# Batch norm with ReLU on one core: two stores of the first tile cut at row 6 instead of row 8

## The chip, the core and the metric

The kernel runs on one core of a Trainium2 chip. The metric is the device time of one execution in microseconds (us); the median of several executions is given with its extremes. All executions quoted here are in the fast state. A ratio is the mean time of one kernel's fast runs over the mean time of the other's fast runs in the same rounds on the same chip, so it is not quite the ratio of the medians quoted beside it.

## The reference

```python
# x: 32 x 128 x 32 x 32, float32; the other inputs: 128 numbers each
normalized = (x - running_mean[None, :, None, None]) / np.sqrt(running_var[None, :, None, None] + eps)
scaled = normalized * gamma[None, :, None, None] + beta[None, :, None, None]
return np.maximum(scaled, 0).astype(np.float32)
```

x has 16.78 MB, and so has the result. Each element is read once and written once.

## The kernel before

Batch and channel are laid out together as 4,096 images of 1,024 numbers (HW in the code). Two tiles (t = 0 and 1) hold 128 partitions x 16 rows; a row is one image, 4 KB in a partition. A channel's scale and bias are worked out once, and one ScalarE activation per row applies them with the ReLU, in place. SyncE, written SP, issues all loads in the first 8.5 us (queue q1). ScalarE issues the stores between its activations (queue q10).

```python
# (t, first row, row after the last): one SBUF tile and one load each, unless LOAD_CUTS cuts the load
TILES = ((0, 0, 2), (0, 2, 4), (0, 4, 8), (0, 8, 16), (1, 0, 16))
LOAD_CUTS = {(1, 8)}
STORE_CUTS = {(0, 1)}
HALVES = {(1, 0), (1, 1)}          # rows whose activation is done in two halves
# ...
with tc.manual_schedule(engines={mybir.EngineType.Activation}):
    for t, a, b, xt in tiles:
        first = a
        for j in range(a, b):
            step = HW // 2 if (t, j) in HALVES else HW
            for w in range(0, HW, step):
                nc.scalar.activation(
                    out=xt[:, j - a, w : w + step], in_=xt[:, j - a, w : w + step], func=ACTF.Relu,
                    bias=bias_t[:, j : j + 1], scale=scale_t[:, j : j + 1],
                )
            if j + 1 == b or (t, j + 1) in STORE_CUTS:
                nc.scalar.dma_start(
                    out=outr[t, :, first : j + 1, :], in_=xt[:, first - a : j + 1 - a, :]
                )
                first = j + 1
```

The rows of one store lie side by side in a partition and in memory, so a store of n rows moves one packet of n x 4 KB per partition. There are 128 packets per store, 8 for each of the 16 DMA engines.

## Time and profile before

| | before |
|---|---|
| time, median of 3 runs | 83.47 us (83.46 to 83.57) |
| span of the instructions in the profile | 81.7 us |
| ScalarE busy | 48% |
| load queue + store queue, share of 16 engines | 48.6% + 47.8% |
| first load packet starts / last store packet ends (packet records) | 1.82 / 80.56 us |

The 16 DMA engines together are called the pipe here. A pipe that carries packets from 1.8 us to 80.6 us and is busy for 96.4% of the span has no idle time in between. Where a text here says "packet records", it means the start, duration and size of each single DMA packet in the trace.

### The profile page before, as it was taken

The numbers are of one execution on the slowest core, as the hardware profiler recorded it, in microseconds if no ns is written. First come the engines' busy times: TensorE is split into PE (matmuls) and PEld (weight loads), VectorE is DVE, ScalarE is ACT, GpSimd is POOL, SyncE is SP. The second block draws the span as 40 slices with busy tenths as digits, with TensorE's granted clock in tenths as the row PEclk, the third lists the DMA queues.
The fourth block names the chain that finished last, engine by engine and source line by source line (L and its number), as shares of the span: only waits on it lengthen the run. The fifth ranks groups of instructions, "written<-read, shape, count | busy, mean of one in ns | idle before, by whom it ended". The sixth has DMA issues, their size and how long they took to land.

```text
span 81.7 us, 128 instructions
## 1 busy us (share of the span) xinstructions
PE 1.7 (2%) x6; PEld 1.5 (2%) x6; DVE 0.8 (1%) x5; ACT 39.1 (48%) x36; POOL 0.8 (1%) x6
## 2 busy tenths in 40 slices
PE   0008000000000000000000000000000000000000
PEld 0007000000000000000000000000000000000000
DVE  0000300000000000000000000000000000000000
ACT  0600477799039999199997199993000000000000
POOL 3000000000000000000000000000000000000000
DMA  2899999989899898969789699996991999998290
GB/s 44 313 422 481 409 481 417 497 369 497 369 385 481 375 491 357 541 293 605 321 373 589 273 489 393 513 497 273 513 770 64 449 513 513 513 513 385 128 513 0
DMA packets 1793, 33.56 MB, mean 411 GB/s; under 512 B 257, under 2 KB 257, under 8 KB 513
## 3 DMA queue, kind: packets, MB, share of 16 engines
q1 hardware_dynamic: 864, 16.78, 48.6%
q10 hardware_dynamic: 928, 16.78, 47.8%
q14 instruction: 1, 0.00, 0.0%
HBM read 16.78 MB, written 16.78 MB: 411 GB/s over the span
## 4 chain that ended last, share of the span: by engine, by line
DMA 56%; ACT 10%; issue 2%; SPq 0%
DMA x<-in_x_dram 56%; ACT x L105 10%; SPq L56 0%
## 5 line engine op out<-in xcount | busy, mean ns | idle before, releaser
L105 ACT ACTIVATE x<-x,bias_t,scale_t 128x1024 f32<-128x1024 f32 (+1 forms) x34 | 37.5, 1178 | 10.0 <-DMA x<-in_x_dram 7.7
L89 ACT ACT_TABLE_LOAD x1 | 1.3, 1283 | 2.7 <-issue 2.7
L89 ACT ACTIVATE std_t<-cols,eps_t 128x16 f32<-128x16 f32 x1 | 0.3, 276 | 4.2 <-PE cols L81 4.2
L81 PE MATMUL cols<-raw,rep 8*128 8x16 f32 (+1 forms) x6 | 1.7, 384 | 6.4 <-DMA raw<-in_gamma_dram 6.3
L81 PEld LDWEIGHTS cols<-raw,rep 8*128 8x128 f32 x6 | 1.5, 307 | 6.5 <-issue 6.3
L68 POOL TENSOR_SCALAR_AFFINE_SELECT rep<-rep 8x128 f32<-8x128 f32 x1 | 0.4, 394 | 0.1
L91 DVE RECIPROCAL rstd_t<-std_t 128x16 f32<-128x16 f32 x1 | 0.3, 253 | 7.5 <-ACT std_t L89 7.5
L67 POOL MEMSET rep<- 8x128 f32 x1 | 0.2, 195 | 0.3 <-POOLq L133 0.3
L93 DVE TENSOR_TENSOR scale_t<-cols,rstd_t 128x16 f32<-128x16 f32 x1 | 0.2, 174 | 0.1
L95 DVE TENSOR_TENSOR ms_t<-cols,scale_t 128x16 f32<-128x16 f32 x1 | 0.2, 174 | 0.0
L97 DVE TENSOR_TENSOR bias_t<-cols,ms_t 128x16 f32<-128x16 f32 x1 | 0.2, 174 | 0.0
L133 POOL MEMSET const-bfloat16-1.0<- 128x1 bf16 x1 | 0.1, 108 | 0.0
L133 POOL MEMSET const-float32-0.0<- 128x1 f32 x1 | 0.1, 105 | 0.3 <-issue 0.3
L133 POOL MEMSET const-uint8-127<- 128x1 uint8 x1 | 0.1, 107 | 0.0
L133 POOL MEMSET const-float32-1.0<- 128x1 f32 x1 | 0.1, 105 | 0.0
L65 DVE MEMSET eps_t<- 128x1 f32 x1 | 0.1, 59 | 0.9 <-PEq L133 0.9
## 6 DMA issues: line engine op xcount, KB each, us to landing
x<-in_x_dram SPq DMA_DIRECT2D x3, 4096.0 KB, 38.6
out_dram<-x ACTq DMA_DIRECT2D x1, 4096.0 KB, 28.6
x<-in_x_dram SPq DMA_DIRECT2D x2, 1024.0 KB, 5.8
x<-in_x_dram SPq DMA_DIRECT2D x1, 2048.0 KB, 11.3
out_dram<-x ACTq DMA_DIRECT2D x1, 2048.0 KB
out_dram<-x ACTq DMA_DIRECT2D x2, 512.0 KB, 19.1
out_dram<-x ACTq DMA_DIRECT2D x1, 1024.0 KB
raw<-in_running_var_dram ACTq DMA_DIRECT2D x1, 0.5 KB
```

What stands on the lines that cost most here:

```text
L65: nc.vector.memset(eps_t, float(eps))
L67: nc.gpsimd.memset(rep, 1.0)
L68: nc.gpsimd.affine_select(out=rep, in_=rep, compare_op=mybir.AluOpType.is_equal, fill=0.0, base=0, pattern=[[0, P // Q], [-1, Q]], channel ...
L81: nc.tensor.matmul(cols[:, a:b, :].rearrange("p k j -> p (k j)"), rep.rearrange("q r s -> q (r s)"), raw[:, a:b, :].rearrange("q k j -> q ...
L89: nc.scalar.activation(out=std_t, in_=cols[:, 0, :], func=ACTF.Sqrt, bias=eps_t[:, 0:1], scale=1.0)
L91: nc.vector.reciprocal(out=rstd_t, in_=std_t)
L93: nc.vector.tensor_mul(out=scale_t, in0=cols[:, 1, :], in1=rstd_t)
L95: nc.vector.tensor_mul(out=ms_t, in0=cols[:, 2, :], in1=scale_t)
L97: nc.vector.tensor_sub(out=bias_t, in0=cols[:, 3, :], in1=ms_t)
L105: nc.scalar.activation(out=xt[:, j - a, w : w + step], in_=xt[:, j - a, w : w + step], func=ACTF.Relu, bias=bias_t[:, j : j + 1], scale=sc ...
L133: nc = _bacc.Bacc("TRN2", target_bir_lowering=False, num_devices=1)
```

## The change

Its intent can be read from the sizes: smaller packets for the store that may meet the last loads, and larger ones for the store that follows. Rows 4 to 15 become one tile, still loaded in two transfers, and its stores are cut after row 5.

```diff
-TILES = ((0, 0, 2), (0, 2, 4), (0, 4, 8), (0, 8, 16), (1, 0, 16))
+TILES = ((0, 0, 2), (0, 2, 4), (0, 4, 16), (1, 0, 16))

-LOAD_CUTS = {(1, 8)}
-STORE_CUTS = {(0, 1)}
+LOAD_CUTS = {(0, 8), (1, 8)}
+STORE_CUTS = {(0, 1), (0, 6)}
```

## The prediction

> **What bounds the kernel now.** I read the page first, then the DMA queues stretch by stretch, then the instructions of ScalarE in order of time.
>
> The page's first two parts, with the queues and the chain:
>
> ```profile
> span 81.7 us, 128 instructions
> ...
> PE 1.7 (2%) x6; PEld 1.5 (2%) x6; DVE 0.8 (1%) x5; ACT 39.1 (48%) x36; POOL 0.8 (1%) x6
> ...
> q1 hardware_dynamic: 864, 16.78, 48.6%
> q10 hardware_dynamic: 928, 16.78, 47.8%
> ...
> DMA 56%; ACT 10%; issue 2%; SPq 0%
> ```
>
> ScalarE, the busiest engine, works 48% of the span. The two DMA queues (q1 loads, issued by SP; q10 stores, issued by ScalarE) keep the 16 DMA engines busy for 48.6 + 47.8 = 96.4% of 81.7 us, which is 78.8 us. The chain gives DMA only 56% because it follows the last instruction of an engine (it ends at 55.9 us with ScalarE), not the store that lands afterwards. So I ask where the other 2.9 us are. The busy time of each stretch, with the DMA share as the last column but one:
>
> ```profile
> core 0: us, PE busy (x) PEld busy (x) DVE busy (x) ACT busy (x) POOL busy (x), PEclk, DMA share, GB/s
> 0.00:1.80 1.80, 0.00 (x0) 0.00 (x0) 0.06 (x1) 0.00 (x0) 0.80 (x6) 1.00 0.00 0
> 1.80:12.10 10.30, 1.75 (x6) 1.49 (x6) 0.78 (x4) 3.76 (x4) 0.00 (x0) 1.00 1.01 407
> ...
> 14.50:46.80 32.30, 0.00 (x0) 0.00 (x0) 0.00 (x0) 24.23 (x24) 0.00 (x0) 1.00 1.01 430
> 46.80:56.00 9.20, 0.00 (x0) 0.00 (x0) 0.00 (x0) 9.12 (x8) 0.00 (x0) 1.00 0.99 427
> 56.00:80.50 24.50, 0.00 (x0) 0.00 (x0) 0.00 (x0) 0.00 (x0) 0.00 (x0) 1.00 0.99 428
> 80.50:81.70 1.20, 0.00 (x0) 0.00 (x0) 0.00 (x0) 0.00 (x0) 0.00 (x0) 1.00 0.00 0
> ```
>
> The share is 0.99 to 1.01 from 1.8 us to 80.5 us; all that is idle is 1.8 us before the first load packet and 1.2 us after the last store packet. (A packet is booked where it starts, hence values a little over 1.) The kernel is a full DMA pipe from one end to the other. A change of store cuts pays only by fewer bytes, fewer or cheaper packets, or by closing a hole, and there is no hole.
>
> Next the packet price. The page counts 1,793 packets, one per partition and row range plus small ones. With stores alone in the pipe, the queue lines of two windows, 46.8 to 51 us (rows 4 to 7, 16 KB each) and 62 to 80 us (the last store, 64 KB each):
>
> ```profile
> DMA packets 112, 1.84 MB, mean 437 GB/s; under 512 B 0, under 2 KB 0, under 8 KB 0
> q10 hardware_dynamic: 112, 1.84, 101.8%
> ...
> DMA packets 112, 7.34 MB, mean 408 GB/s; under 512 B 0, under 2 KB 0, under 8 KB 0
> q10 hardware_dynamic: 112, 7.34, 94.0%
> ```
>
> 1.018 x 4.2 us x 16 / 112 = 0.611 us for a 16 KB packet, and 0.940 x 18 us x 16 / 112 = 2.417 us for one of 64 KB. The trace's single packet records agree and give all sizes of the store queue: 4 KB 0.159, 8 KB 0.309, 16 KB 0.611, 32 KB 1.213, 64 KB 2.418 us. The line from 32 to 64 KB has a slope of 1.205 us per 32,768 bytes (27.2 GB/s an engine, 435 GB/s for 16), and leaves about 0.008 us per packet whatever its size.
>
> **What the Trainium skill says.** "DMA: Bandwidth & Descriptors", section "Where 436 GB/s comes from", puts the ceiling of 16 engines at 435.2 GB/s; the slope above is that figure, so the bytes already flow at the ceiling. The same page, section "Queues, rings and completion order", says that each engine round-robins between its queue rows one packet at a time. The trace agrees: while loads of 32 KB and stores of 4 KB share the pipe (26 to 34 us), q1 has 88 packets at 82.8% and q10 has 89 at 11.1%: one for one by number, so a store's share grows with its packet. This is the one mechanism by which other cuts could move the loads. Section "Why small descriptors are slow (HBM only)" gives a fixed cost per packet; here it is the 0.008 us above, negligible from 4 KB up.
>
> **The change part by part.** The instruction streams of the two programs compare so: ScalarE keeps 34 activations and 6 stores, SP its 6 loads with the same sizes (2 x 8, 16, 3 x 32 KB a partition). Rows 4 to 15 become one tile loaded by two transfers; the activation of row 8 alone waits for the second, so the first four rows do not wait longer. Two things move: the store of 16 KB packets, issued after row 7, becomes one of 8 KB packets issued after row 5; that of 32 KB becomes 40 KB, issued after row 15 as before. One SP wait changes: the load of tile 1's first half waits for the beta load instead of the mean load before it is issued.
>
> *Bytes and packets.* Each engine sends 8 packets per store. Before: 8 x (0.611 + 1.213) = 14.59 us. After: 8 x 0.309 = 2.47 us for rows 4 and 5, and 8 x (40,960 bytes / 27.2 GB/s + 0.008) = 8 x 1.514 = 12.11 us, together 14.58 us. Difference: 0.01 us, nothing. The packets number 128 x 2 in both.
>
> *Order in the pipe.* The instructions of ScalarE in order of time:
>
> ```profile
> 15.61 4.63 ACT L105 ACTIVATE x<-x,bias_t,scale_t 128x1024 f32<-128x1024 f32 x4 [0.42 <-ACT x L105]
> 20.27 0.34 ACTq L113 DMA_DIRECT2D out_dram<-x  x1
> 23.84 9.16 ACT L105 ACTIVATE x<-x,bias_t,scale_t 128x1024 f32<-128x1024 f32 x8 [3.59 <-DMA x<-in_x_dram]
> 33.02 0.34 ACTq L113 DMA_DIRECT2D out_dram<-x  x1
> ...
> 46.77 9.16 ACT L105 ACTIVATE x<-x,bias_t,scale_t 128x1024 f32<-128x1024 f32 x8 [2.27 <-DMA x<-in_x_dram]
> 55.95 0.34 ACTq L113 DMA_DIRECT2D out_dram<-x  x1
> ```
>
> The store of rows 4 to 7 is issued at 20.27 us, but in the packet records its first packet starts at 46.35 us, 26 us later. Until then the store queue works through row 0 (from 14.56 us), row 1 (to 34.56 us) and rows 2 and 3 (36.56 to 46.69 us), one packet of theirs for each 32 KB load packet. The last load packets end at 46.07 us. So the two re-cut stores start where the loads end. Issuing rows 4 and 5 at about 18 us instead of 20.27 gains nothing, because they stand behind rows 0 to 3 either way; and their packets meet no load packet that they could push aside. Everything up to 46.4 us should stay, including the landing at 46.77 us that releases the last eight activations.
>
> *ScalarE.* One store issue moves from after row 7 to after row 5: about 0.4 us earlier in the list (0.34 us for the issue and the gap round it). Rows 6 and 7 end 0.4 us later, near 20.6 us; the next load lands at 23.8 us, so the 3.59 us of idle time absorb it. The issue at 33.02 us stays.
>
> *After the loads.* Before, from 46.69 us: 14.59 us of stores take the pipe to 61.3 us (the 32 KB packets end at 61.24 us in the records), and the last store, issued at 55.95 us, follows without a hole for 8 x 2.418 = 19.34 us, to 80.55 us. After: 14.58 + 19.34 us from the same start, to the same end. The sum of all parts is 0.0 us.
>
> **The rivals.** *A hole before the last store.* If the pipe drained before 55.95 us, the time would grow by the hole. The stores queued at 46.7 us last until 61.3 us in both kernels, 5.3 us beyond that issue. Between them, the 40 KB store must be there when rows 4 and 5 run out, at 46.7 + 2.5 = 49.2 us; it is issued at 33 us, 16 us early. Against it; 83.5 us stays.
>
> *Later loads through larger store packets.* Had the 40 KB packets run beside loads, eight of them would have cost 12.1 us where the 32 KB ones cost 9.7 us, and the last load would slip by 2.4 us. By the order above no re-cut store runs there; and a slip would first eat the 5.3 us of queued stores, still leaving 83.5 us.
>
> *The 40 KB packet is not priced on the line.* No packet of that size runs in the kernel before. If it were cut into 32 + 8 KB it would cost 1.522 instead of 1.514 us, 8 x 0.008 = 0.06 us in all. To be 2% slower (1.67 us) the 5.2 MB would have to run 14% below the rate that all five other sizes show; I see no sign of it, but this is the untested point: at worst 85.2 us.
>
> *The changed semaphore.* Beta lands about 0.6 us after the mean (7.46 against 6.83 us in the semaphore records), so tile 1's first load is issued at 7.5 instead of 6.84 us. It is needed in the pipe only when the load before it runs out, past 23 us. SP's following load waits for a landing at 8.10 us anyway. Hidden.
>
> **Range and chances.** The time before is 83.47 us (83.46 to 83.57 in three runs), and the sum of the parts is 0.0 us. I keep 83.45 us with a margin of some 0.25 us on each side for packet order at the seams and for the chip's run-to-run spread: 83.2 to 83.7 us. Only an unforeseen price of the 40 KB packet or a hole could reach 2%, and I found nothing that could take 1.67 us off a pipe that is 96.4% full, with the rest lying at its two ends. Chances: 0.01 faster, 0.98 same, 0.01 slower.
>
> **What would show it right or wrong.** In the changed kernel's profile: the two queues again add up to about 78.8 us; the DMA share stays near 1 between 1.8 and 80.5 us; the 8 KB and 40 KB packets of the re-cut stores start after about 46 us and take 0.309 and 1.514 us; the last eight activations start near 46.8 us; the last store is issued near 56.0 us, well before the 40 KB packets end near 61.2 us. It is wrong if a share near 0 appears anywhere after 2 us, if the 40 KB packets take over 1.6 us, or if the last load lands later by more than 5 us.

## The result

| | before | changed |
|---|---|---|
| time, median of 4 runs | 83.49 us (83.46 to 83.57) | 83.53 us (83.48 to 83.55) |
| ratio | | 1.0002 (0.9985 to 1.0019) |

The times are the same. The changed kernel's page, its span and queues:

```profile
span 81.8 us, 128 instructions
...
q1 hardware_dynamic: 864, 16.78, 48.6%
q10 hardware_dynamic: 928, 16.78, 47.7%
```

The queues add up to 96.3% of 81.8 us, 78.8 us, as before. The busy time of three stretches (the DMA share is the last column but one):

```profile
0.00:1.80 1.80, 0.00 (x0) 0.00 (x0) 0.06 (x1) 0.00 (x0) 0.80 (x6) 1.00 0.00 0
1.80:80.50 78.70, 1.75 (x6) 1.49 (x6) 0.78 (x4) 39.18 (x36) 0.00 (x0) 1.00 1.00 426
80.50:81.80 1.30, 0.00 (x0) 0.00 (x0) 0.00 (x0) 0.00 (x0) 0.00 (x0) 1.00 0.00 0
```

The share is 1.00 over 78.7 us; the idle time lies only at the two ends. ScalarE's instructions in order of time (start, duration, then what; ACTq is its queue issuing a DMA):

```profile
15.48 2.37 ACT L105 ACTIVATE x<-x,bias_t,scale_t 128x1024 f32<-128x1024 f32 x2 [0.42 <-ACT x L105]
17.88 0.34 ACTq L113 DMA_DIRECT2D out_dram<-x  x1
18.27 2.37 ACT L105 ACTIVATE x<-x,bias_t,scale_t 128x1024 f32<-128x1024 f32 x2 [0.42 <-ACT x L105]
23.95 9.16 ACT L105 ACTIVATE x<-x,bias_t,scale_t 128x1024 f32<-128x1024 f32 x8 [3.31 <-DMA x<-in_x_dram]
33.14 0.34 ACTq L113 DMA_DIRECT2D out_dram<-x  x1
...
46.88 9.16 ACT L105 ACTIVATE x<-x,bias_t,scale_t 128x1024 f32<-128x1024 f32 x8 [2.27 <-DMA x<-in_x_dram]
56.06 0.34 ACTq L113 DMA_DIRECT2D out_dram<-x  x1
```

The store of rows 4 and 5 is issued at 17.88 us, 2.4 us before the old store of rows 4 to 7 was. Every later time shown is 0.1 us later than before. The packet records give the price of the re-cut packets: all 128 of 40 KB took 1.514 us, and all of 8 KB in the store queue took 0.309 us. The first 40 KB packet started at 48.84 us, after the last load packet (46.18 us).

### The profile page after: what moved, and what is told of

The parts are those of the page before. It is cut to its first block, busy times and chain, and to the rows that moved or that the text cites. A ratio compares the mean times of both kernels' runs of the same rounds, so it can differ in the third digit from the quotient of the medians.

```text
span 81.8 us, 128 instructions
## 1 busy us (share of the span) xinstructions
PE 1.8 (2%) x6; PEld 1.5 (2%) x6; DVE 0.8 (1%) x5; ACT 39.2 (48%) x36; POOL 0.8 (1%) x6
## 4 chain that ended last, share of the span: by engine, by line
DMA 56%; ACT 10%; issue 2%; SPq 0%
DMA x<-in_x_dram 56%; ACT x L105 10%; SPq L56 0%
```

## The experiments

**Theory.** The pipe is full until its last packet. A store cut can cost or gain only by the price of its packets, by a hole (a stretch in which the pipe is idle), or by pushing the loads back far enough to make a hole later; the change does none of these. **Rivals.** (a) Large packets or odd sizes have a price of their own, and something else in the change paid for it. (b) The time at which a store is issued matters by itself. (c) The order and the cuts never matter in this kernel. Twelve kernels ran, all with correct results. The kernel before, run beside each batch on the same chip, took 83.46 us (first four), 83.53 us (next three), 83.52 us (next four) and 83.50 us (last).

### One store of rows 4 to 15

```diff
-STORE_CUTS = {(0, 1), (0, 6)}
+STORE_CUTS = {(0, 1)}
```

> Rows 4 to 15 go out in one store of 48 KB packets, issued after row 15 (near 33 us). Theory (the pipe is full and these stores stand behind rows 0 to 3 until the loads end near 46 us): no hole and no slip of the loads, 83.5 us (83.3 to 83.7), 48 KB packets of 49,152 bytes / 27.2 GB/s + 0.008 = 1.816 us. Rival (sizes off the powers of two, or over 40 KB, cost more per byte, or the early store of rows 4 and 5 is needed): slower by over 0.5 us.

Measured: 83.86 us (83.81 to 84.0), ratio 1.0053 (1.0037 to 1.007). The forecast of the time missed. Inside the trace all that the theory said is there: 48 KB packets of 1.815 us, no hole, and the last packet ends at 80.54 us (80.56 in the kernel before). The page's first line gives the span:

```profile
span 81.8 us, 126 instructions
```

Of the 0.4 us more, 0.34 us lie outside the span: the profiled run's time less its span was 2.05 us, against 1.71 us in the kernels before and changed. The other runs agree: 2.0 to 2.1 us in all four, 1.7 to 1.8 us in the seven of the kernel before beside them. The rival's 0.4 us were thus real as a time, and not in the pipe. The last group of experiments follows this up.

### The 40 KB store issued after row 7 of tile 1, and after row 12

```diff
+HOLD = {(0, 6): (1, 7)}           # second kernel: {(0, 6): (1, 12)}
...
-                    nc.scalar.dma_start(out=outr[t, :, first : j + 1, :], in_=xt[...])
+                    store = (outr[t, :, first : j + 1, :], xt[...])
+                    held.setdefault(HOLD.get((t, first), (t, j)), []).append(store)
                     first = j + 1
+                for dst, tile_rows in reversed(held.pop((t, j), [])):
+                    nc.scalar.dma_start(out=dst, in_=tile_rows)
```

> The changed kernel with the 40 KB store issued only after row 7 of tile 1, near 44.6 us instead of 33.1 us. Theory (the pipe needs this store only when rows 4 and 5 run out, at 49.2 us): 11.5 us of delay cost nothing, 83.5 us (83.3 to 83.8). Rival (the time of issue itself sets the end): slower by up to 11.5 us.

> The same store held until after row 12 of tile 1, near 52.6 us. Theory: rows 4 and 5 run out at 49.2 us, the first 40 KB packet comes 1.0 to 1.5 us after the issue (the first load took 1.0 us), so a hole of about 4.5 us with DMA share near 0 and a time of 88.0 us (87.3 to 88.7). Rival (the end is set by something other than the pipe, such as ScalarE, whose last store stays near 56 us): 83.5 us.

Measured: 83.57 us (83.46 to 83.67), ratio 1.0013, and 83.43 us (83.42 to 83.46), ratio 0.9998. The second forecast missed, because the hold did not hold. The second kernel's ScalarE in order of time:

```profile
46.74 1.24 ACT L108 ACTIVATE x<-x,bias_t,scale_t 128x1024 f32<-128x1024 f32 x1 [2.27 <-DMA x<-in_x_dram]
46.75 0.34 ACTq L120 DMA_DIRECT2D out_dram<-x  x1
47.89 8.01 ACT L108 ACTIVATE x<-x,bias_t,scale_t 128x1024 f32<-128x1024 f32 x7
55.93 0.34 ACTq L120 DMA_DIRECT2D out_dram<-x  x1
```

In the program the 40 KB store stands behind five activations, of rows 8 to 12. It was issued at 46.75 us, 0.01 us after the first of the five began. The other four, of rows 9 to 12, began only at 47.89 us and later. In the first kernel the store stands behind ten activations and was issued at 34.86 us, not 44.6 us: 0.04 us after the first of the ten, which waits for a load, began at 34.82 us. So in both kernels the issue passed activations that had not begun, but not one that still waited for its load: the rows that this store waits for had been done since 33 us, and it was issued in neither kernel before that load was in. So these two runs tell only that a delay from 33.1 to 46.75 us, 13.6 us, is free, which is what the theory says of any issue early enough for 49.2 us.

### The 40 KB store behind a store that truly waits for row 12

```diff
-STORE_CUTS = {(0, 1), (0, 6)}
+STORE_CUTS = {(0, 1), (0, 6), (1, 13)}   # on top of HOLD = {(0, 6): (1, 12)}
```

> The earlier hold after row 12 did not hold: its store was issued at 46.75 us, while the activations of rows 9 to 12 were still to run. Here the last store is cut after row 12, so that a store which truly waits for row 12 (near 52.6 us) stands in front of the 40 KB store. Theory: the pipe is empty from 49.2 us to 1.0 to 1.5 us after that issue, a hole of about 4.6 us, and the rest follows without a hole: 88.1 us (87.3 to 88.8). Rival (the pipe has slack elsewhere that takes up the hole): 83.5 us.

Measured: 88.27 us (88.19 to 88.34), ratio 1.0568 (1.0554 to 1.0581). ScalarE in order of time, at the two issues together:

```profile
52.52 0.82 ACTq L120 DMA_DIRECT2D out_dram<-x  x2
```

The busy time of the stretches round it, with the DMA share as the last column but one:

```profile
46.80:49.20 2.40, 0.00 (x0) 0.00 (x0) 0.00 (x0) 2.40 (x3) 0.00 (x0) 1.00 0.83 352
49.20:53.30 4.10, 0.00 (x0) 0.00 (x0) 0.00 (x0) 3.29 (x3) 0.00 (x0) 1.00 0.00 0
53.30:85.10 31.80, 0.00 (x0) 0.00 (x0) 0.00 (x0) 3.50 (x3) 0.00 (x0) 1.00 1.00 429
```

The packets of rows 4 and 5 end at 49.11 us and the next packet starts at 53.36 us, 0.84 us after the issue. The last packet ends at 85.14 us, against 80.66 us in the changed kernel: 4.5 us later, of which the hole is 4.25 us. So a hole goes into the time nearly one for one, and nothing takes it up. (This kernel also has a seventh store, since the last one is cut in 52 and 12 KB.) Together with the two runs above it shows where the limit lies: an issue at 46.75 us costs nothing, one at 52.5 us costs 4.7 us.

### The same bytes in 4 KB pieces

Rows 4 to 15 are written to a second tile whose rows stand 64 bytes apart, so their two stores can't be one run per partition.

```diff
+    padded = data.tile([P, 12, HW + 16], F32, name="padded")
...
+            yt = padded if (t, a) == (0, 4) else xt
-                        out=xt[:, j - a, w : w + step],
+                        out=yt[:, j - a, w : w + step],
-  ... in_=xt[:, first - a : j + 1 - a, :]
+  ... in_=yt[:, first - a : j + 1 - a, 0:HW]
```

> The changed kernel, but rows 4 to 15 are written to a second tile whose rows stand 64 bytes apart, so their two stores break into 4 KB pieces: 96 per engine instead of 16. Theory (0.008 us per piece): 96 x 0.159 = 15.26 us in place of 14.58 us, all of it in the full pipe, so 83.5 + 0.7 = 84.2 us (84.0 to 84.4). Rival (a piece has no price of its own in a full pipe): 83.5 us.

Measured: 83.94 us (83.86 to 83.95), ratio 1.0056 (1.0041 to 1.0071). The store queue from 50 to 60 us:

```profile
DMA packets 1030, 4.22 MB, mean 422 GB/s; under 512 B 0, under 2 KB 0, under 8 KB 1030
q10 hardware_dynamic: 1030, 4.22, 102.4%
```

1.024 x 10 us x 16 / 1,030 = 0.159 us each, the recorded duration that the line gives. The packet records sum to 15.27 us per engine for the two stores, 0.69 us more than 14.58 us, as worked out. The time rose by 0.0056 x 83.5 = 0.47 us (0.34 to 0.59), clear of the rival's zero but under the forecast of 84.0 to 84.4 us. In the profiled runs the last packet ends at 80.98 us against 80.56 us in the kernel before. So a packet does have a price of its own, but the forecast of the time was 0.2 us too high. The lines above show where these went: 1,030 packets in 10 us on 16 engines is a start every 0.155 us on each, less than the 0.159 us that a packet is recorded to take. The records overlap by 0.003 to 0.004 us, which is why the share is over 100%. By the starts in the packet records a 16 KB packet costs 0.607 us (recorded 0.611), one of 32 KB 1.209 (1.213), of 40 KB 1.511 (1.514), of 64 KB 2.414 (2.418). That leaves about 0.005 us per packet and not 0.008, and 80 packets more cost an estimated 0.4 us, within the measured 0.34 to 0.59. The change itself keeps the number of packets, so this price doesn't enter it.

### The 40 KB packets beside the loads

Same six stores, other order: rows 0 to 3 are issued after the 40 KB store, with the HOLD code above.

```diff
+HOLD = {(0, 0): (0, 15), (0, 1): (0, 15), (0, 2): (0, 15)}
```

> The changed kernel with the same six stores in another order: rows 0 to 3 are issued after the 40 KB store, so rows 4 and 5 and then the 40 KB packets run beside the loads. Theory (one store packet for one load packet): about seven rounds of 1.213 + 1.514 us stand before the end of the loads, the last load lands near 54 us (52 to 56) instead of 46.9, the last store is issued near 63 us, the queued stores are out near 61 us, so a hole of some 3.5 us and 86.7 us (85.5 to 88.5). Rival (a full pipe does not care which store runs when): 83.5 us.

Measured: 88.17 us (88.09 to 88.39), ratio 1.0563 (1.0543 to 1.0582). Both queues from 44 to 50 us:

```profile
q1 hardware_dynamic: 42, 1.38, 53.1%
q10 hardware_dynamic: 32, 1.31, 50.5%
```

ScalarE in order of time:

```profile
55.51 9.16 ACT L108 ACTIVATE x<-x,bias_t,scale_t 128x1024 f32<-128x1024 f32 x8 [10.59 <-DMA x<-in_x_dram]
64.69 0.34 ACTq L120 DMA_DIRECT2D out_dram<-x  x1
```

The busy time of three stretches, DMA share as above:

```profile
60.00:61.50 1.50, 0.00 (x0) 0.00 (x0) 0.00 (x0) 1.50 (x3) 0.00 (x0) 1.00 0.88 358
61.50:65.50 4.00, 0.00 (x0) 0.00 (x0) 0.00 (x0) 3.17 (x3) 0.00 (x0) 1.00 0.00 0
65.50:85.00 19.50, 0.00 (x0) 0.00 (x0) 0.00 (x0) 0.00 (x0) 0.00 (x0) 1.00 1.00 430
```

The queues take turns packet by packet: in the packet records 96 packets of each start between 36.8 and 52.5 us, so the 40 KB stores, at 1.514 us each against 1.23 us for a load packet, take a little over half of the pipe. ScalarE waits 10.59 us for the last load and goes on at 55.51 us instead of 46.88 us; the last store is issued at 64.69 us, the queued stores end at 61.59 us, and the next packet starts at 65.54 us, a hole of 3.95 us. The theory's size was low: it put the time at 86.7 us, though the measured one lies inside its range. Its 54 us for the last load fits the data, whose last packet ends at 53.61 us, but ScalarE goes on 0.38 us after the load queue's last 4-byte packet, which follows the data and ends at 55.13 us, later by as much as a 40 KB packet takes. In the changed kernel these two packets end at 46.18 and 46.49 us. Rival (c) has fallen: the same stores in a bad order cost 4.6 us.

### Rows 0 and 1 in one store, with the new cuts and with the old

```diff
-STORE_CUTS = {(0, 1), (0, 6)}      # changed kernel
+STORE_CUTS = {(0, 6)}
-STORE_CUTS = {(0, 1)}              # kernel before
+STORE_CUTS = set()
```

> The changed kernel with rows 0 and 1 in one store of 8 KB packets: 8 packets per engine and one store fewer. Theory: 8 x 0.008 us and a completion less, about 0.08 us; rows 4 and 5 now run beside the last loads, which land 2.4 us later (near 49.2 us), the last store is issued near 58.4 us, still before the queued stores run out at 61.2 us. So 83.4 us (83.2 to 83.6), not to be told from 83.5. Rival (a later last load moves the end): 85.9 us.

> The kernel before with rows 0 and 1 in one store of 8 KB packets, so that its 16 KB store of rows 4 to 7 runs beside the last loads. Theory: the loads land 16 x 0.309 + 8 x 0.611 - 5.0 = 4.8 us later (near 51.5 us), the last store is issued near 60.7 us, and with 1.0 to 1.5 us to its first packet it misses the end of the queued stores at 61.2 us: a hole of 0.3 to 1.2 us, 84.2 us (83.7 to 84.7), slower than the same edit to the changed kernel. Rival (cuts never matter in this kernel): 83.4 us for both.

Measured: 84.18 us (84.05 to 84.29), ratio 1.0075 (1.0062 to 1.0088), with the new cuts; 84.3 us (84.26 to 84.37), ratio 1.0093 (1.0079 to 1.0107), with the old. By these intervals the two are not told apart, although the medians stand in the order that was forecast. In the traces they do differ; ScalarE's last two lines with the new cuts, then with the old:

```profile
49.24 9.16 ACT L105 ACTIVATE x<-x,bias_t,scale_t 128x1024 f32<-128x1024 f32 x8 [2.39 <-DMA x<-in_x_dram]
58.43 0.34 ACTq L113 DMA_DIRECT2D out_dram<-x  x1
...
51.12 9.16 ACT L105 ACTIVATE x<-x,bias_t,scale_t 128x1024 f32<-128x1024 f32 x8 [4.29 <-DMA x<-in_x_dram]
60.31 0.34 ACTq L113 DMA_DIRECT2D out_dram<-x  x1
```

The new cuts' last eight activations start at 49.24 us and the last store is issued at 58.43 us, with the queued stores out at 61.56 us. The old cuts' start at 51.12 us, with the last store at 60.31 us and the queued stores out at 61.64 us. So the smaller packets of rows 4 and 5 do give the loads 1.9 us, once they meet them. Neither kernel has a hole, for 60.31 us plus the 0.84 us from issue to first packet is just in time: the first 64 KB packet starts at 61.34 us. The old cuts' time fits its range for another reason than the hole it was put down to, and the new cuts' time missed its range by 0.58 us. In both, the time less the span was 2.06 us, which is again 0.35 us outside the span; the rest of the loss, 0.3 to 0.4 us, is inside it.

### What the 0.35 us outside the span go with

The three kernels with it have 55 recorded instructions of ScalarE (a store and a wait fewer); those without it have 57. Two activations of half a row more bring 55 back to 57, in time that ScalarE waits for the last load anyway.

```diff
-HALVES = {(1, 0), (1, 1)}
+HALVES = {(1, j) for j in range(4)}      # third kernel: range(8)
```

> The kernel with one store of rows 4 to 15, whose time was 0.4 us over its span's promise, with two more activations of half a row in ScalarE's idle time, which brings ScalarE's recorded instructions from 55 back to 57. Theory (the 0.4 us are a price outside the span that goes with the number of ScalarE's instructions: 1.71 us at 57, 1.87 at 56, 2.05 at 55): 83.5 us, time less span 1.71 us. Rival (the merged store itself costs 0.4 us, or the number of stores sets the price): 83.86 us, time less span 2.05 us.

> The changed kernel with the same two more activations: 59 instructions of ScalarE. If the price outside the span falls by 0.17 us per instruction without end: 83.2 us, time less span 1.37 us. If 57 is where it levels off, or it goes in steps of some block: 83.5 us and 1.71 us, or a step up.

> The changed kernel with six more activations of half a row: 63 instructions of ScalarE. Straight line: 82.5 us, time less span 0.7 us. Levelled off: 83.5 us and 1.71 us. ScalarE's extra 1 us lies in the 2.3 us that it waits for the last load, so the span stays at 81.8 us in both.

> The changed kernel with rows 0 and 1 in one store, again with two more activations of half a row, so that ScalarE has 57 recorded instructions instead of 55. If all of that kernel's extra 0.65 us were the price outside the span: 83.5 us. Theory: 0.34 us of it are outside the span and go, and 0.3 us are inside (its 32 KB load packets took 1.233 us on average against 1.221 in the kernel before) and stay: 83.85 us, span 82.1 us.

| kernel | ScalarE records | time, median | ratio to before | profiled run: time less span |
|---|---|---|---|---|
| one store of rows 4 to 15 | 55 | 83.86 us | 1.0053 | 2.05 us |
| the same, 4 rows in halves | 57 | 83.53 us (83.5 to 83.72) | 1.0004 | 1.72 us |
| rows 0 and 1 in one store | 55 | 84.18 us | 1.0075 | 2.06 us |
| the same, 4 rows in halves | 57 | 83.71 us (83.69 to 83.84) | 1.0028 | 1.71 us |
| rows 0 to 3 last | 56 | 88.17 us | 1.0563 | 1.87 us |
| changed, 4 rows in halves | 59 | 83.6 us (83.37 to 83.81) | 1.0015 | 1.70 us |
| changed, 8 rows in halves | 63 | 83.59 us (83.47 to 83.72) | 1.0007 | 1.84 us |

The merged store costs nothing once ScalarE's stream has its old length: 83.53 us, with its 48 KB packets unchanged. The number of stores does not set the price either: the profiled runs with 57 instructions have 1.71 to 1.72 us outside the span with five, six or seven stores. The straight line has fallen: 59 and 63 instructions gain nothing. Nor does the price simply level off: of the six runs with 59, three have 1.7 us outside the span and three 1.9 to 2.0 us, and all five with 63 have 1.8 us. What sets it stays open; the runs show only that two instructions more take it away from two of the three kernels with 55. One hint, not tested: in the trace with 63 an 8 KB packet of the instruction queue (q14) starts at 82.96 us, after the span; no other kept trace has one there.

Of the 0.65 us of the kernel with rows 0 and 1 in one store, the last run leaves 0.23 us (0.0028 x 83.5); its 83.71 us lies between the two forecasts. They lie in the pipe, whose last packet ends at 80.76 us against 80.56 us in the kernel before; the spans of its five runs are 82.0 to 82.1 us against 81.7 to 81.9 us. The expectation put them down to its 32 KB load packets, which took 1.230 us on average against 1.221 us. That is not shown: in the changed kernel they took 1.229 us, without such a cost. The cause stays open.

No kernel of these beats the two.

## Why the prediction was right

*The bound.* The prediction took the pipe as full from 1.8 to 80.5 us, with idle time only at the ends. The profile after shows a share of 1.00 over that stretch. The kernel with the hole shows that the pipe does set the end: 4.25 us of it raised the time by 4.7 us.

*Bytes and packets.* 14.58 us were worked out for the two re-cut stores. The packet records sum to 8 x 0.309 + 12.11 = 14.58 us. The 40 KB packet, the one size without a record before, took 1.514 us as predicted from the line. The 48 KB packet lies on it too (1.815 us). The constant of that line is too high, though: from start to start a packet costs 0.003 to 0.004 us less than its record says, so about 0.005 us remain per packet and not 0.008, as the 4 KB pieces show. It cancels here, because both kernels send as many packets. It also accounts for a slip in the sum: 46.69 + 14.59 + 19.34 is 80.62 us and not the 80.55 us that the prediction wrote and the records show.

*Order in the pipe.* The first 40 KB packet was to start once the loads were out: 48.84 us against 46.18 us. The last eight activations start at 46.88 us (predicted 46.8), the last store at 56.06 us (predicted 56.0), and the 40 KB packets end at 61.34 us (predicted 61.2). That this order was a condition and not a matter of course is shown by the kernel with rows 0 to 3 last.

*ScalarE and the changed wait.* Rows 6 and 7 end at 18.27 + 2.37 = 20.64 us (predicted near 20.6), and the idle time that follows is 3.31 instead of 3.59 us. The first load of tile 1 is issued at 7.35 us instead of 6.84 (predicted 7.5), and ScalarE's first activation on it starts at 34.89 instead of 34.78 us, no later than the general 0.1 us.

*The rivals.* "A hole before the last store" was rejected by a margin of 16 us at the 40 KB store; the held stores used 13.6 us of it without cost, and one that overran it cost the overrun. "Later loads through larger store packets" was rejected on order alone, which holds. The added claim that a slip would first eat 5.3 us of queued stores also holds: the kernel before with rows 0 and 1 in one store slipped by 4.3 us (46.77 to 51.12 us) without a hole, and the one with rows 0 to 3 last by 8.6 us, against the changed kernel, with one. But the 5.3 us were too many: from the issue of a store to its first packet pass 0.84 us, so by these numbers about 4.4 us could be used.

The prediction did not see the term outside the span. That it didn't need to was luck: both kernels have 57 instructions of ScalarE and 1.71 us outside the span. For one store of rows 4 to 15 the same reasoning gave 83.3 to 83.7 us, and the measured 83.86 us lies above.

## What to carry to other kernels

Before judging a re-cut of transfers, find the DMA share of each stretch: where it is 1 from the first packet to the last, as here, look first to bytes, packet count and holes for what can move the end. Then find when each store's first packet runs, not when it is issued, and how long the queued stores last past the issue of the last one, less the time from issue to first packet (0.84 us here). This is the slack; in these runs delays and slips within it made no hole. When a time moves and the span doesn't, or not as much, compare time less span before explaining anything inside.

## What the Trainium skill lacked or had wrong

- "DMA: Bandwidth & Descriptors", section "Queues, rings and completion order": it says that an engine drains a packet before it changes queues, and takes a packet to be about 9 to 17 descriptors. The records here show one packet per contiguous run of a partition, up to 64 KB, and the queues change after each: 96 packets of 32 KB loads and 96 of 40 KB stores start between 36.8 and 52.5 us of the kernel with rows 0 to 3 last. So the length of the run sets a queue's share. No section gives the fixed time of a packet of 4 KB or more; here it is about 0.005 us from start to start (0.008 us by recorded durations).
- "Perfetto Trace Analysis", section "DVE / Act Engine Instruction (TENSOR_ADD, Activation, etc)": there the sequencer pushes an activation and goes on. A store issued at 46.75 us, ahead of four activations that stand before it in the program and had not begun, agrees. The section does not warn that program order alone therefore doesn't hold a DMA back, nor say why this store, whose own wait had been met since 33 us, still stayed until the activation that waited for its load began at 46.74 us.
- "Runtime: NRT & Kernel Launch", section "The ~15µs preamble/postamble breakdown", has fixed stages around a kernel. It has no cost that changes with small edits of one engine's instruction stream: here 1.71 us outside the span with 57 recorded instructions of ScalarE, 1.87 us with 56, 2.05 us with 55 and 1.84 us with 63.
